# Attention on one core: folding the running maximum to 64 partitions, and where its transposes stand

## The chip, the cores and the metric

The kernel runs on one core of one Trainium2 chip. The metric is the device time of one execution in microseconds (us). The kernel before takes 1297.36 us (median of three runs, 1296.2 to 1297.93). The profile was taken from one further execution, which took 1299.13 us; its span, from the first instruction to the last, is 1296.9 us.

## The reference

The reference is one encoder layer with two groups of token mixing heads over a sequence of 2048 tokens of width 1024: gated linear attention (group A), multi-head latent attention with four heads (group B), one output projection over both, a residual and a layer norm. The change touches group B alone, whose core is a softmax over all 2048 keys:

```python
def attend(blk):
    qn, qr = blk
    s = (jnp.einsum('bqhd,bkhd->bhqk', qn, k_nope, preferred_element_type=jnp.float32)
         + jnp.einsum('bqhr,bkr->bhqk', qr, k_r, preferred_element_type=jnp.float32))
    p = jax.nn.softmax(s, axis=-1)
    return jnp.einsum('bhqk,bkhv->bqhv', p.astype(v.dtype), v)
```

The softmax subtracts, for each query, the largest score over all keys before the exponential.

## The kernel before

Three stages follow one another: group A (about 0 to 470 us of the span), then chunks of projections that overlap it (to about 605 us), then `attention` (L1501), which ends in the output projection, the residual and the layer norm.

**Blocks and pairs.** Attention runs 16 blocks i = 0 to 15, each one head by 512 queries. A block has 8 pairs j = 0 to 7 of key tiles, 2 x 128 keys each. Scores are held with keys on the partitions and queries along the row, so a maximum over keys is a maximum over partitions. Numbers are split into a high and a low part, so that a product takes several matmuls.

For each pair:

- `scores` (L1527, products on L1535 to L1539): ten products on TensorE into a PSUM tile `pS` of two banks. There are two such tiles, so the scores of pair j + 2 can't start until pair j's tile has been read.
- `copy` (L1541): ScalarE copies the tile to SBUF.
- `smax` (L1546, L1554 and L1557): VectorE folds the two halves of the PSUM tile into the running maximum `rm`, 128 partitions by 512 queries. Of the readers of the tile it is the last.
- `sub`, `exp`, `phi`, `plo` (L1578 to L1592): VectorE subtracts the maximum, ScalarE takes the exponential and copies the high part, GpSimd makes the low part `pl`.
- `pv` (L1615): six products of weights and values into `o`.
- `acc` (L1602): half of the pairs are summed on VectorE into `ap`, the others on GpSimd.

Once per block:

- `tmax` (L1559): four TensorE transposes of `rm` into the one-bank PSUM pool `pX`; `rmax` (L1565): one VectorE reduction of them to `mc`; `bmax` (L1570): four TensorE transposes that spread `mc` over all partitions into `mb`, which each `sub` reads.
- `tot`, `own_half`, `fold`, `tsum`, `rcp` (L1625 to L1660): the same for the sum. Here ScalarE copies half of the sum to the other 64 partitions (`own_half`, two instructions of 64 x 256), VectorE adds the halves (`fold`, two of 64 x 256), and only two transposes follow. `keep` stores the reciprocals with a DMA of ScalarE's queue.
- `oh`, `ol`, `y`, `yc` (L1689 to L1706): the block's output is split and multiplied by a value matrix into a tile of `pX`; ScalarE evacuates it and a DMA of SyncE's queue stores it.
- For block 14 `turn` (L1676) takes the place of `keep`: one small transpose of the reciprocals into `pX` on TensorE, then `rows` (L1683), a ScalarE copy and a DMA on SyncE's queue.

**The order is written out by hand.** Every step of every block is put on one list with a place, and the list is sorted. `scores` of pair j of block i has place 8i + j; the other steps of a pair are that place plus the value in `PLACE` (L74); those of a block are 8i + 7 plus it. `PLACE_LAST` (L100) holds for block 15, `PLACE_OUT` for the steps of the output projection. `in_order` (L386) chains each engine's instructions, the DMA queues' included, in exactly this order. So an instruction that waits holds up all that stand behind it on its engine.

Around a block's end, before the change, the list reads (next block's pairs are called p0 to p7): scores of p0; maximum of pair 7; sum of pair 5 on VectorE; `tmax`; value products of pair 4 of the block before; `rmax`; `bmax`; a `phi`; copy of p0; scores of p1; maximum of p0; value products of pair 5; three `sub`; then `tot`, maximum of p1, one `sub`, `fold`, maximum of p2, two `sub`, `ol`, maximum of p3.

Of the kernel before, what the change touches and what calls it, by code (L numbers as in the profile page):

```python
# [9 lines left out]
F32 = mybir.dt.float32  # L10
F32R = mybir.dt.float32r
I32 = mybir.dt.int32
AF = mybir.ActivationFunctionType
ALU = mybir.AluOpType
AX = mybir.AxisListType
# [3 lines left out]
P = 128  # L19
# [8 lines left out]
QB = 512  # L28
# [45 lines left out]
PLACE = dict(  # L74
    copy=0.73,
    max=1.21,
    sub=(9.47, 8.65, 7.39, 7.37, 7.49, 6.63, 6.95, 7.44),
    exp=(10.18, 9.95, 7.63, 9.15, 8.26, 9.12, 7.84, 8.01),
    hi=(10.39, 10.41, 9.81, 10.32, 9.82, 10.74, 10.53, 10.47),
    lo=(11.99, 11.22, 11.21, 12.62, 11.98, 11.51, 10.87, 10.63),  # L80
    pv=(12.35, 12.1, 11.89, 12.65, 12.27, 12.25, 12.14, 11.45),
    acc=(12.45, 11.78, 12.32, 0, 10.57, 11.24, 10.03, 9.22),
    acc0=10.78,
    tmax=1.26,
    rmax=1.27,
    bmax=1.48,
    tot=11.2,
    half=11.7,
    fold=11.95,
    tsum=12.37,  # L90
    rcp=13.55,
    keep=14.21,
    turn=13.6,
    rows=13.65,
    oh=12.34,
    ol=12.99,
    y=16.55,
    yc=16.9,
)
PLACE_LAST = dict(  # L100
    sub=(9.67, 8.74, 8.38, 6.77, 10.45, 3.53, 9.53, 5.55),
    exp=(10.14, 9.35, 10.49, 8.31, 13.01, 14.59, 17.1, 18.05),
    hi=(10.43, 11.83, 12.21, 14.39, 15.18, 22.96, 28.7, 34.03),
# [256 lines left out]
class K:  # L360
# [1140 lines left out]
    def attention(self):  # L1501
        tc, nc = self.tc, self.nc
        mm = nc.tensor.matmul
        V, G, Ac = nc.vector, nc.gpsimd, nc.scalar
        NP = NKT // 2
        with ExitStack() as ctx:
# [4 lines left out]
            pM, pO, pX, pA, pS = bank("pM"), bank("pO"), bank("pX"), bank("pA"), bank("pS", 2)  # L1511
            blocks = [(h, b) for b in range(NQB) for h in range(H)]
            nb = len(blocks)
            stt = [dict(s=[None] * NP) for _ in blocks]
# [31 lines left out]
            def smax(i, j):  # L1546
# [8 lines left out]
                else:  # L1555
                    for e in range(2):
                        V.tensor_tensor(d["rm"], src[:, e], d["rm"], ALU.max)  # L1557

            def tmax(i):  # L1559
                d = stt[i]  # L1560
                d["x"] = pX.tile([P, 4, P], F32, tag="x", name=f"mx{i}")
                for e in range(4):
                    nc.tensor.transpose(d["x"][:, e], d["rm"][:, e * P:(e + 1) * P], self.ident)

            def rmax(i):  # L1565
                d = stt[i]
                d["mc"] = op.sm.tile([P, 4], F32, tag="mc", name=f"mc{i}")
                V.tensor_reduce(d["mc"], d["x"], AX.X, ALU.max)

            def bmax(i):  # L1570

# [53 lines left out]
            def tot(i):  # L1625
# [4 lines left out]
                    return  # L1630
                for e in range(2):
                    V.tensor_tensor(d["ap"], d["ap"], d["as"][:, e], ALU.add)

            halves = [(slice(64 * e, 64 * e + 64), slice(64 - 64 * e, 128 - 64 * e), slice(e * QB // 2, (e + 1) * QB // 2))
                      for e in range(2)]

            def own_half(i):
                d = stt[i]
# [88 lines left out]
            def put(place, fn, *a):  # L1727
                todo.append((place, len(todo), fn, a))

            def at(f, i, j=None):  # L1730
                p = PLACE_LAST.get(f, PLACE[f]) if i == nb - 1 else PLACE[f]
                return p[j] if isinstance(p, tuple) else p

            own = (("tot", tot), ("half", own_half), ("fold", fold), ("tsum", tsum), ("rcp", rcp), ("keep", keep), ("oh", oh), ("ol", ol), ("y", y), ("yc", yc))
            own_late = tuple(e for e in own if e[1] is not keep) + (("turn", turn), ("rows", rows))
            for i in range(nb):
                for j in range(NP):
                    t = NP * i + j
                    put(t, scores, i, j)
                    for n, f in (("copy", copy), ("max", smax), ("sub", sub), ("exp", exp), ("hi", phi), ("lo", plo),  # L1740
                                 ("pv", pv), ("acc", acc)):
                        if n != "acc" or j != SUM_POOL[0] or i == nb - 1:
                            put(t + at(n, i, j), f, i, j)
                put(NP * i + at("acc0", i), acc0, i)
                for n, f in (("tmax", tmax), ("rmax", rmax), ("bmax", bmax)) + {nb - 1: (), nb - 2: own_late}.get(i, own):
                    put(NP * i + NP - 1 + at(n, i), f, i)
                if i + 2 < nb:
                    put(NP * i + 4.05, fetch, i + 2)
# [300 lines left out]
```

## Time and profile before

| What | us |
|---|---|
| median of three runs | 1297.36 |
| the profiled execution | 1299.13 |
| its span | 1296.9 |
| TensorE busy, 0 to 470 us of the span | 457.44 |
| TensorE busy, 470 to 605 us | 133.93 |
| TensorE busy, 605 to 1090 us (blocks 0 to 15) | 483.08 |
| VectorE busy in that stretch | 423.74 |
| ScalarE busy in that stretch | 404.42 |
| GpSimd busy in that stretch | 408.72 |
| TensorE busy, 1090 to 1297 us (output) | 195.76 |

Busy time is the time in which an engine had an instruction running. Matmuls overlap, so the start of one to the start of the next says more than the duration of one. PE is TensorE's matmul, PEld its weight load, DVE is VectorE, ACT ScalarE, POOL GpSimd, SPq SyncE's queue. A timeline row holds the start, the duration, the engine, the line, the operation, output and inputs, the shapes and a count of merged instructions; a bracket at its end gives the idle time just before it and who ended that.

### The profile page before, as it was taken

Reading aid. Unit: us, or ns where it says so; the run is one execution under the profiler, and the core shown is the slowest. Engines: PE = TensorE matmul, PEld = TensorE weight load, DVE = VectorE, ACT = ScalarE, POOL = GpSimd, SP = SyncE. Lnnn points to the kernel's source line nnn. Section 1 sums busy time; section 2 is a strip of 40 time slices with the busy share of each in tenths; the row PEclk is TensorE's granted clock in tenths of the full one; section 3 lists DMA queues with packets and bytes.
Section 4 is the critical chain, followed back from the end, with each engine's and each line's share of the span. In section 5 each row is a group of like instructions: output and inputs, shape, how many; then the busy total and the mean of one; then the engine's idle time right before and its main releaser. Section 6 shows DMA issues by size and latency. Waiting matters only on the chain.

```text
span 1296.9 us, 19995 instructions
## 1 busy us (share of the span) xinstructions
PE 1270.2 (98%) x6988; PEld 1119.6 (86%) x6988; DVE 908.5 (70%) x1678; ACT 842.7 (65%) x1482; POOL 790.9 (61%) x500
## 2 busy tenths in 40 slices
PE   7999999999999999999999999999999999999997
PEld 7999999999889999999788888888888888788886
DVE  6865564445675455555898888888888888468655
ACT  7765657555675656655688888888888887523221
POOL 0243232232567666671288888889999999846550
PEclk9999999999999999999999999999999999999999
DMA  8232213131565555565401111122233110367752
GB/s 287 70 94 59 88 55 93 51 96 50 179 224 170 193 200 179 189 213 168 138 1 41 42 41 41 41 63 60 58 90 90 42 41 9 122 197 238 238 170 75
DMA packets 113444, 145.81 MB, mean 112 GB/s; under 512 B 17494, under 2 KB 70110, under 8 KB 113344
## 3 DMA queue, kind: packets, MB, share of 16 engines
q1 hardware_dynamic: 105184, 142.42, 34.9%
q0 software_dynamic: 768, 2.10, 0.4%
q8 instruction: 55, 0.90, 0.3%
q10 hardware_dynamic: 7392, 0.03, 0.3%
q14 instruction: 45, 0.37, 0.1%
HBM read 94.14 MB, written 50.36 MB: 111 GB/s over the span
## 4 chain that ended last, share of the span: by engine, by line
PE 86%; ACT 3%; DVE 2%; POOL 2%; issue 2%; DMA 1%; SPq 0%; DVEq 0%; ACTq 0%; POOLq 0%
PE o L424 4%; PE o L426 4%; PE pS L1535 4%; PE o L425 4%; PE pS L1537 4%; PE pS L1536 4%; PE pS L1538 4%; PE pS L1539 4%; PE ipa L424 4%; PE ipa L426 3%; PE ipa L425 3%; PE po L426 2%; PE po L425 2%; PE po L424 2%; PE pz L425 2%; PE pz L426 2%
## 5 line engine op out<-in xcount | busy, mean ns | idle before, releaser
L376 POOL TENSOR_TENSOR pl<-s,ph 128x1024 fp32r<-128x1024 f32 x128 | 306.3, 2417 | 58.0 <-ACT ph L370 58.0
L1557 DVE TENSOR_TENSOR rm<-pS,rm 128x512 f32<-128x512 f32 x210 | 144.8, 690 | 26.3 <-ACT s L1544 20.7
L1581 DVE TENSOR_TENSOR s<-s,mb 128x1024 f32<-128x1024 f32 x128 | 151.2, 1213 | 9.4 <-PE mb L1575 9.3
L1544 ACT ACTIVATE s<-pS 128x1024 f32<-128x1024 f32 x128 | 131.3, 1026 | 38.0 <-PE pS L1539 33.4
L1044 POOL TENSOR_TENSOR Us<-Us,cw 128x512 f32<-128x512 f32 x16 | 18.6, 1164 | 213.1 <-DVE Us L1042 181.3
L370 ACT ACTIVATE ph<-s 128x1024 fp32r<-128x1024 f32 x128 | 135.2, 1058 | 17.6 <-PE o L426 16.9
L1585 ACT ACTIVATE s<-s 128x1024 f32<-128x1024 f32 x128 | 131.5, 1051 | 13.4 <-DVE s L1581 13.3
L424 PE MATMUL ipa<-wah,xah 128*128 128x384 f32 (+1 forms) x384 | 131.1, 341 | 7.3 <-ACT wah L370 6.8
L425 PE MATMUL ipa<-wal,xah 128*128 128x384 f32 (+1 forms) x384 | 125.8, 327 | 0.2 <-DVE wal L376 0.2
L426 PE MATMUL ipa<-wah,xal 128*128 128x384 f32 (+1 forms) x384 | 125.0, 325 | 0.0
L1535 PE MATMUL pS<-qh,ckvT_h 128*128 128x512 f32 x256 | 102.5, 401 | 0.8 <-DVE rm L1557 0.4
L424 PE MATMUL o<-ph,vh 128*128 128x512 f32 x256 | 101.0, 395 | 0.0
L1536 PE MATMUL pS<-ql,ckvT_h 128*128 128x512 f32 x256 | 99.8, 390 | 0.0
L1538 PE MATMUL pS<-rh,krs 128*128 128x512 f32 x256 | 99.8, 390 | 0.0
L1537 PE MATMUL pS<-qh,ckvT_l 128*128 128x512 f32 x256 | 99.8, 390 | 0.0
L426 PE MATMUL o<-ph,vl 128*128 128x512 f32 x256 | 99.8, 390 | 0.0
L1539 PE MATMUL pS<-rl,krs 128*128 128x512 f32 x256 | 99.8, 390 | 0.0
L425 PE MATMUL o<-pl,vh 128*128 128x512 f32 x256 | 99.7, 390 | 0.0
L1608 DVE TENSOR_TENSOR ap<-ap,s 128x512 f32<-128x512 f32 x120 | 83.1, 692 | 7.1 <-ACT s L1585 4.5
L424 PEld LDWEIGHTS ipa<-wah,xah 128*128 128x128 f32 x384 | 73.1, 190 | 10.4 <-ACT wah L370 7.0
L376 POOL TENSOR_TENSOR ol<-of,oh 128x512 fp32r<-128x512 f32 x32 | 43.6, 1363 | 54.2 <-ACT oh L370 54.2
L424 PE MATMUL pz<-xch,wzh 128*128 128x256 f32 x256 | 74.8, 292 | 0.0
(327 smaller groups left out, 3830.1 us busy)
## 6 DMA issues: line engine op xcount, KB each, us to landing
xcf<-xT_dram SPq DMA_DIRECT2D x16, 512.0 KB, 5.3
xr<-x_dram SPq DMA_DIRECT2D x16, 512.0 KB, 5.7
out_dram<-rr SPq DMA_DIRECT2D x32, 256.0 KB, 4.9
xaf<-xT_dram SPq DMA_DIRECT2D x14, 512.0 KB, 3.8
oib<-oi_s SPq DMA_DIRECT2D x16, 256.0 KB, 3.8
qdb<-qd_s SPq DMA_DIRECT2D x16, 256.0 KB, 4.9
SU<-su_s SPq DMA_DIRECT2D x16, 256.0 KB, 4.1
ub<-u_s SPq DMA_DIRECT2D x16, 256.0 KB, 4.1
```

The source lines that it names most:

```text
L370: return nc.scalar.activation(dst, src, AF.Copy).ins
L376: return e.tensor_tensor(dst, src, hi.bitcast(F32), ALU.subtract).ins
L424: mm(out, ah, bh, start=start, stop=False)
L425: mm(out, ah, bl, start=False, stop=False)
L426: mm(out, al, bh, start=False, stop=stop)
L1535: mm(ps[:, e], kh, qh, start=True, stop=False)
L1536: mm(ps[:, e], kh, ql, start=False, stop=False)
L1537: mm(ps[:, e], kl, qh, start=False, stop=False)
L1538: mm(ps[:, e], kr, rh, start=False, stop=False)
L1539: mm(ps[:, e], kr, rl, start=False, stop=True)
L1557: V.tensor_tensor(d["rm"], src[:, e], d["rm"], ALU.max)
L1581: V.tensor_tensor(s, s, d["mb"][:, None, :].to_broadcast([P, 2, QB]), ALU.subtract)
```

## The change

For blocks 1 to 14 the running maximum is folded, as the sum already was. `hmax`: ScalarE copies half of `rm` (two instructions of 64 x 256) into the unused half of the PSUM tile of `pX`. `fmax`: VectorE takes the maximum of both halves (two instructions of 64 x 256). `tmax` then makes two transposes instead of four, and `rmax` reduces 256 instead of 512 columns. Blocks 0 and 15 keep the old form and the old places.

The places of the folded blocks move. `tmax` goes from 1.26 to 1.9, behind the six value products at 1.27. `bmax` goes from 1.48 to 2.2, behind the ten score products of p1, which stand between the two. `turn` and `rows` of block 14 move from 13.6 and 13.65 to 17.5 and 17.55: behind 24 output products, `y`, `yc` and the first six value products of block 15.

```diff
-    tmax=1.26,
-    rmax=1.27,
-    bmax=1.48,
+    hmax=1.45,
+    fmax=1.65,
+    tmax=1.9,
+    rmax=1.91,
+    bmax=2.2,
...
-    turn=13.6,
-    rows=13.65,
+    turn=17.5,
+    rows=17.55,
...
+PLACE_FIRST = dict(
+    tmax=1.26,
+    rmax=1.27,
+    bmax=1.48,
+)
 PLACE_LAST = dict(
+    tmax=1.26,
+    rmax=1.27,
+    bmax=1.48,
...
+            folded = lambda i: 0 < i < nb - 1
+
+            def other_half(i):
+                d = stt[i]
+                d["x"] = pX.tile([P, 4, P], F32, tag="x", name=f"mx{i}")
+                f = d["x"][:, 2:4].rearrange("p a t -> p (a t)")
+                for own_p, other_p, qs in halves:
+                    Ac.activation(f[own_p], d["rm"][other_p, qs], AF.Copy)
+
+            def fold_max(i):
+                d = stt[i]
+                f = d["x"][:, 2:4].rearrange("p a t -> p (a t)")
+                for own_p, _, qs in halves:
+                    V.tensor_tensor(d["rm"][own_p, :QB // 2], f[own_p], d["rm"][own_p, qs], ALU.max)
+
             def tmax(i):
                 d = stt[i]
-                d["x"] = pX.tile([P, 4, P], F32, tag="x", name=f"mx{i}")
-                for e in range(4):
+                if not folded(i):
+                    d["x"] = pX.tile([P, 4, P], F32, tag="x", name=f"mx{i}")
+                for e in range(2 if folded(i) else 4):
                     nc.tensor.transpose(d["x"][:, e], d["rm"][:, e * P:(e + 1) * P], self.ident)
 
             def rmax(i):
                 d = stt[i]
                 d["mc"] = op.sm.tile([P, 4], F32, tag="mc", name=f"mc{i}")
-                V.tensor_reduce(d["mc"], d["x"], AX.X, ALU.max)
+                if not folded(i):
+                    V.tensor_reduce(d["mc"], d["x"], AX.X, ALU.max)
+                else:
+                    V.tensor_reduce(d["mc"].rearrange("p (e j) -> p j e", e=2),
+                                    d["x"][:, 0:2].rearrange("p j (e k) -> p j e k", e=2), AX.X, ALU.max)
...
+                fmax = (("hmax", other_half), ("fmax", fold_max)) if folded(i) else ()
+                for n, f in fmax + (("tmax", tmax), ("rmax", rmax), ("bmax", bmax)) + {nb - 1: (), nb - 2: own_late}.get(i, own):
                     put(NP * i + NP - 1 + at(n, i), f, i)
```

More of the change, by code (lines that the diff above doesn't have):

```diff
@@ L1557, in smax @@
                         V.tensor_tensor(d["rm"], src[:, e], d["rm"], ALU.max)
+            halves = [(slice(64 * e, 64 * e + 64), slice(64 - 64 * e, 128 - 64 * e), slice(e * QB // 2, (e + 1) * QB // 2))
+                      for e in range(2)]
+            folded = lambda i: 0 < i < nb - 1
[10 more added lines that the diff above has]
+                    V.tensor_tensor(d["rm"][own_p, :QB // 2], f[own_p], d["rm"][own_p, qs], ALU.max)
             def tmax(i):
                 d = stt[i]
-                d["x"] = pX.tile([P, 4, P], F32, tag="x", name=f"mx{i}")
-                for e in range(4):
+                if not folded(i):
+                    d["x"] = pX.tile([P, 4, P], F32, tag="x", name=f"mx{i}")
+                for e in range(2 if folded(i) else 4):
                     nc.tensor.transpose(d["x"][:, e], d["rm"][:, e * P:(e + 1) * P], self.ident)
@@ L1632, in tot @@
                     V.tensor_tensor(d["ap"], d["ap"], d["as"][:, e], ALU.add)
-            halves = [(slice(64 * e, 64 * e + 64), slice(64 - 64 * e, 128 - 64 * e), slice(e * QB // 2, (e + 1) * QB // 2))
-                      for e in range(2)]
             def own_half(i):
@@ L1730, in at @@
             def at(f, i, j=None):
-                p = PLACE_LAST.get(f, PLACE[f]) if i == nb - 1 else PLACE[f]
+                p = PLACE_LAST.get(f, PLACE[f]) if i == nb - 1 else PLACE_FIRST.get(f, PLACE[f]) if i == 0 else PLACE[f]
                 return p[j] if isinstance(p, tuple) else p
@@ L1744, in attention @@
                 put(NP * i + at("acc0", i), acc0, i)
-                for n, f in (("tmax", tmax), ("rmax", rmax), ("bmax", bmax)) + {nb - 1: (), nb - 2: own_late}.get(i, own):
+                fmax = (("hmax", other_half), ("fmax", fold_max)) if folded(i) else ()
+                for n, f in fmax + (("tmax", tmax), ("rmax", rmax), ("bmax", bmax)) + {nb - 1: (), nb - 2: own_late}.get(i, own):
                     put(NP * i + NP - 1 + at(n, i), f, i)
```

## The prediction

> **What bounds the kernel now.** I read the page's busy times first, then TensorE's waits, then the timeline of one attention block on TensorE and on VectorE.
>
> ```profile
> PE 1270.2 (98%) x6988; PEld 1119.6 (86%) x6988; DVE 908.5 (70%) x1678; ACT 842.7 (65%) x1482; POOL 790.9 (61%) x500
> ```
>
> TensorE bounds the whole: 98% busy. So a change pays only if it takes slots from TensorE, and costs as soon as TensorE waits. TensorE around the end of block 6 (p0 to p7 are the next block's pairs; the first column is the start in us of the span):
>
> ```profile
> 813.89 0.60 PE L1563 MATMUL mx<-ident,rm 128*128 128x128 f32 x4
> ...
> 815.02 0.40 PE L424 MATMUL o<-ph,vh 128*128 128x512 f32 x1
> ...
> 815.72 0.60 PE L1575 MATMUL mb<-ident,mc 128*128 128x128 f32 x4
> ...
> 819.80 0.39 PE L1535 MATMUL pS<-qh,ckvT_h 128*128 128x512 f32 x1
> ...
> 824.79 0.39 PE L1535 MATMUL pS<-qh,ckvT_h 128*128 128x512 f32 x1
> ...
> 827.06 0.38 PE L1658 MATMUL sx<-ident,acc 128*128 128x128 f32 x2
> 827.19 0.48 PE L1535 MATMUL pS<-qh,ckvT_h 128*128 128x512 f32 x1
> 828.43 0.39 PE L1535 MATMUL pS<-qh,ckvT_h 128*128 128x512 f32 x1
> ...
> 830.95 0.39 PE L1535 MATMUL pS<-qh,ckvT_h 128*128 128x512 f32 x1
> ...
> 835.94 0.39 PE L1535 MATMUL pS<-qh,ckvT_h 128*128 128x512 f32 x1
> ...
> 844.78 0.60 PE L1563 MATMUL mx<-ident,rm 128*128 128x128 f32 x4
> ```
>
> No row has a bracket: TensorE never waits here. The scores of p2, p3, p4, p5, p6 start at 819.80, 824.79, 827.19, 830.95, 835.94. Ten products take 2.27 (824.79 to 827.06), so one takes 0.227. VectorE in the same stretch:
>
> ```profile
> 812.23 1.42 DVE L1608 TENSOR_TENSOR ap<-ap,s 128x512 f32<-128x512 f32 x2
> 814.52 0.69 DVE L1568 TENSOR_REDUCE mc<-mx 128x4 f32<-128x512 f32 x1 [0.87 <-PE mx L1563]
> ...
> 816.42 3.48 DVE L1581 TENSOR_TENSOR s<-s,mb 128x1024 f32<-128x1024 f32 x3 [0.59 <-PE mb L1575]
> 819.82 1.43 DVE L1632 TENSOR_TENSOR ap<-ap,acc 128x512 f32<-128x512 f32 x2
> 821.16 1.41 DVE L1557 TENSOR_TENSOR rm<-pS,rm 128x512 f32<-128x512 f32 x2
> 822.48 1.21 DVE L1581 TENSOR_TENSOR s<-s,mb 128x1024 f32<-128x1024 f32 x1
> 823.71 0.86 DVE L1646 TENSOR_TENSOR acc<-ap,acc 64x256 f32<-64x256 f32 x2
> 824.59 1.42 DVE L1557 TENSOR_TENSOR rm<-pS,rm 128x512 f32<-128x512 f32 x2
> 825.93 2.34 DVE L1581 TENSOR_TENSOR s<-s,mb 128x1024 f32<-128x1024 f32 x2
> 828.19 0.68 DVE L376 TENSOR_TENSOR ofl<-o,ofh 128x512 fp32r<-128x512 f32 x1
> 828.79 1.41 DVE L1557 TENSOR_TENSOR rm<-pS,rm 128x512 f32<-128x512 f32 x2
> ...
> 833.70 2.93 DVE L1557 TENSOR_TENSOR rm<-pS,rm 128x512 f32<-128x512 f32 x4
> ...
> 839.53 1.42 DVE L1557 TENSOR_TENSOR rm<-pS,rm 128x512 f32<-128x512 f32 x2 [0.45 <-ACT s L1544]
> ```
>
> From the first subtraction (816.42, which waits for the broadcast `mb`) to the maximum of p3 VectorE has no idle time at all. And the maxima of p1, p2, p3 (L1557) stand in that run: each frees the score tile that p3, p4 and p5 write. Here is a second, hidden clock of the block, and it starts with the broadcast.
>
> **The change part by part.**
>
> *Two transposes fewer.* Four transposes and three value products take 815.02 - 813.89 = 1.13; the three products are 0.68, so the four cost 0.45. Two transposes and five products take 828.43 - 827.06 = 1.37, less 1.13 leaves 0.24. The fold saves 0.21 of TensorE per block, over blocks 1 to 14 **-3.0 us**. Bounds: nothing to 0.45 a block.
>
> *Broadcast ten products later.* Now `mb` starts at 815.72 and the first subtraction 0.70 behind it. On TensorE the scores of p2 and all later work stay in their order behind `mb`; only p1's ten products come to stand ahead of it. Against the scores of p2 and later, VectorE's run therefore starts 2.27 later. How late a score waits once a maximum has ended can be read where block 0 ends, since there VectorE is already late:
>
> ```profile
> 638.00 1.41 DVE L1557 TENSOR_TENSOR rm<-pS,rm 128x512 f32<-128x512 f32 x2
> ```
> ```profile
> 639.55 0.47 PE L1535 MATMUL pS<-qh,ckvT_h 128*128 128x512 f32 x1 [0.42 <-DVE rm L1557]
> 639.86 0.40 PE L1536 MATMUL pS<-ql,ckvT_h 128*128 128x512 f32 x1
> ```
>
> The maximum ends at 639.41; the second product starts at 639.86, so the stream resumes as if at 639.63: 0.22 after the end. With 2.27 + 0.22 = 2.49 added to the end of each maximum:
>
> - p3 needs p1's maximum: 821.16 + 1.41 + 2.49 = 825.06 against 824.79: 0.27 late.
> - p4 needs p2's: 824.59 + 1.42 + 2.49 = 828.50 against 827.19: 1.31 late.
> - p5 needs p3's: 828.79 + 1.41 + 2.49 = 832.69 against 830.95: **1.74 late**.
> - p6 needs p4's, half of the four at 833.70: 835.17 + 2.49 = 837.66 against 835.94: 1.72, within the 1.74 already lost.
>
> So TensorE loses 1.74 per block in three waits of about 0.3, 1.0 and 0.4. Before the change the same check leaves 830.95 - 830.42 = 0.53 of slack at p5, which is why no bracket shows. By the maximum of p6, which today has idle time ahead of it (0.45, waiting for a copy), VectorE is paced by TensorE again; the loss does not build up, but each block pays it anew. Over 14 blocks **+24.4 us**. With the release at 0 instead of 0.22 it would be 1.52, with 0.5 it would be 2.0 a block.
>
> *The fold itself.* It adds two copies on ScalarE and two maxima on VectorE, of the shapes of these groups:
>
> ```profile
> L1646 DVE TENSOR_TENSOR acc<-ap,acc 64x256 f32<-64x256 f32 x4 | 1.7, 421 | 0.1
> L1640 ACT ACTIVATE acc<-ap 64x256 f32<-64x256 f32 x4 | 1.5, 371 | 0.0
> ```
> ```profile
> 812.18 1.06 ACT L370 ACTIVATE ph<-s 128x1024 fp32r<-128x1024 f32 x1
> ...
> 814.08 1.03 ACT L1544 ACTIVATE s<-pS 128x1024 f32<-128x1024 f32 x1 [0.84 <-PE pS L1539]
> ```
>
> The copies (0.74) go ahead of the high part at 812.18, and ScalarE has 0.84 idle behind it, so p0's copy keeps its time, by 0.1. While they wait they hold that high part and p0's copy, which p0's maximum needs only behind the reduction. On VectorE the sum ends at 812.23 + 1.42 = 813.65; the two maxima (0.84) end at 814.49, with the release 814.71. The transposes now stand six products (1.36) behind 813.89, at 815.25: 0.5 to spare. The reduction starts 0.63 behind the transposes (814.52 - 813.89) and takes at most 0.69: 816.6, and the broadcast stands at 815.25 + 0.24 + 2.27 = 817.8. VectorE, waiting for it, has nothing else in its order but p0's maximum. I cost the fold at nothing; without the cover it is up to 0.84 a block.
>
> *The small transpose of block 14.*
>
> ```profile
> 1101.62 0.40 PE L1658 MATMUL sx<-ident,acc 128*128 128x128 f32 x2
> 1105.28 0.27 PE L1680 MATMUL rt<-ident,rc 128*4 128x128 f32 x1 [3.26 <-DVE rc L1669]
> ...
> 1109.61 0.51 PE L424 MATMUL y<-ofh,wv_h 128*128 128x512 f32 x1
> ```
> ```profile
> 1103.90 0.69 DVE L376 TENSOR_TENSOR ofl<-o,ofh 128x512 fp32r<-128x512 f32 x1 [1.00 <-ACT ofh L370]
> ```
> ```profile
> 1106.00:1110.00 4.00, 4.00 (x13) 3.10 (x12) 3.97 (x6) 2.04 (x3) 2.38 (x1) 0.57 0.38 132
> ```
>
> It waits 3.26 for the reciprocal, and then the granted clock (third column from the right) is 0.57. Between 1101.62 and `y` at 1109.61 lie two transposes and twelve products, 0.24 + 2.72 = 2.96 of work in 7.99. Moved back, the products start at once; `y` is then due at 1104.6, its operand ends at 1104.59 and is released by 1104.8. Gain 1109.61 - 1104.8 = **-4.8 us**; bounds 3.3 (the wait alone) and 5.0.
>
> The Trainium skill, "TensorE: Matmul & The Clock Gate", section "What's actually happening", says that an idle window of about 3.4 us halves TensorE's clock and that sustained work restores it. The 0.57 behind 3.26 agrees; by it both parts of the gain go together.
>
> Its reciprocal's store moves on SyncE's queue too:
>
> ```profile
> 1105.88 0.27 SPq L1687 DMA_DIRECT2D r_s<-rt  x1
> 1106.24 0.35 SPq L1848 DMA_DIRECT2D wof<-wO_dram  x1
> ```
>
> The next weight load stood right behind it and comes earlier, which helps `yc`, whose tile the transpose must now wait for.
>
> **Sum:** 24.4 - 3.0 - 4.8 = +16.6 us, on the profiled execution 1299.1 + 16.6 = 1315.7. That execution lies 1.8 above the median of the runs; on the median the forecast is **1314 us**. About 0.2%, 2.6 us, is what a measurement of this kernel can tell from no change.
>
> **The rivals.**
>
> *The lateness is absorbed, faster (0.07).* If p5's scores had at least 2.27 + 0.22 of slack behind p3's maximum, only the savings stay: 1297.4 - 3.0 - 4.8 = 1289.6. It decides at the maximum of p3: today's slack is 0.75 before the release, and VectorE's run has no gap to close. Against it speaks also that block 0's end shows this very wait. For it: the three idle brackets of VectorE show that over a whole block it has time.
>
> *The fold is late (0.08).* If the copies wait behind more of ScalarE's work, the two transposes wait as well. The point is the 0.5 to spare; a fold 1.0 late costs 0.5 a block, 7 us more: 1321. For it: ScalarE's margin is 0.1.
>
> *The short waits lower the clock (0.04).* If three waits per block had the effect of the 3.26 one, each block would run some 4 us at 0.57, 1.7 more, 14 x 1.7 = 24: 1338. Against:
>
> ```profile
> 632.00:644.00 12.00, 10.08 (x46) 7.58 (x46) 10.66 (x13) 9.11 (x10) 2.89 (x2) 1.00 0.11 35
> ```
>
> TensorE is idle for 1.9 of these 12 us in several short waits, and the clock granted is 1.00. The Trainium skill, same page, section "A second HAM failure mode: psum-queue depth-cycling", describes just this: frequent short idle times between groups of matmuls that cycle PSUM make the clock go down and up. It speaks against the change; the row does not bear it out.
>
> *The fold saves nothing, or the waits are shorter (0.03).* Without the 3.0 it is 1317; with half of the delay hidden, 1302.
>
> **How the numbers follow.** My forecast, waits at p3 to p5, has 0.78. Its own range: 1.52 to 2.0 lost, 0.45 to 0 saved per block, 3.3 to 5.0 at the end, gives 1.07 x 14 - 5.0 = +10 to 2.0 x 14 - 3.3 = +24.7, that is 1307 to 1322. I reach up a little for a late fold and down for part of a hidden delay: 1305 to 1324. Faster 0.07, same 0.02, slower 0.91.
>
> **What would show it.** After the change TensorE's waits should name scores (L1535's group) released by VectorE's `rm`, some 14 times three, about 24 us together. From one `mx` to the next it is 30.9 us now (813.89 to 844.78) and should be 32.4. VectorE's idle time ahead of the first subtraction should grow from 0.59 to about 1.5. The wait at `rt` and the 0.57 should be gone. I am wrong if TensorE shows no such waits, if `mx` or `mb` waits, or if the clock falls in the blocks.

## The result and the profile after

The changed kernel takes **1315.5 us** (median of four runs, 1314.9 to 1316.9) against 1297.3 for the kernel before (also four runs): a ratio of 1.0143, with a 95% interval of 1.0128 to 1.0158. The forecast was 1314, range 1305 to 1324. The profiled execution's span is 1315.1, 18.2 more than the 1296.9 before.

The busy times, from the first line of the profile's page:

```profile
PE 1277.8 (97%) x6960; PEld 1112.0 (85%) x6960; DVE 915.5 (70%) x1706; ACT 850.2 (65%) x1510; POOL 791.0 (60%) x500
```

There are 28 matmuls fewer, and yet the span is longer. The list of TensorE's waits (total us, times, longest) holds two groups that are new in this size. Before, the scores waited for a maximum once, 0.4 us, at the end of block 0, and that wait is still among the 15; the value products waited for nothing:

```profile
PE pS L1545 <- DVE rm L1567: 10.1, 15, 0.7
...
PE o L434 <- DVE ofl L386: 3.3, 14, 0.3
```

Line numbers are 10 to 33 higher than before: L1545 is the first score product, L434 the first of a value product, L1592 the transposes of the maximum (`mx`), L1608 the broadcast (`mb`). Here is TensorE's timeline of one block, with the same rows that the prediction shows of the kernel before and the first value product:

```profile
822.82 0.38 PE L1592 MATMUL mx<-ident,rm 128*128 128x128 f32 x2
...
825.33 0.60 PE L1608 MATMUL mb<-ident,mc 128*128 128x128 f32 x4
...
827.16 0.39 PE L1545 MATMUL pS<-qh,ckvT_h 128*128 128x512 f32 x1
...
832.32 0.47 PE L1545 MATMUL pS<-qh,ckvT_h 128*128 128x512 f32 x1
...
834.70 0.38 PE L1688 MATMUL sx<-ident,acc 128*128 128x128 f32 x2
835.77 0.47 PE L1545 MATMUL pS<-qh,ckvT_h 128*128 128x512 f32 x1 [0.69 <-DVE rm L1567]
...
838.53 0.50 PE L434 MATMUL o<-ph,vh 128*128 128x512 f32 x1 [0.25 <-DVE ofl L386]
...
840.02 0.39 PE L1545 MATMUL pS<-qh,ckvT_h 128*128 128x512 f32 x1
...
845.06 0.39 PE L1545 MATMUL pS<-qh,ckvT_h 128*128 128x512 f32 x1
...
855.26 0.38 PE L1592 MATMUL mx<-ident,rm 128*128 128x128 f32 x2
```

The broadcast now stands behind p1's products, and from one `mx` to the next it takes 32.44 us where it took 30.89 (the forecast was 32.4). Counted from the start of p2's scores, the later pairs start:

| scores of | before | after | later by | forecast |
|---|---|---|---|---|
| p3 | 4.99 | 5.16 | 0.17 | 0.27 |
| p4 | 7.39 | 8.61 | 1.22 | 1.31 |
| p5 | 11.15 | 12.86 | 1.71 | 1.74 |
| p6 | 16.14 | 17.90 | 1.76 | 1.74 |

VectorE in the same block:

```profile
826.03 3.48 DVE L1614 TENSOR_TENSOR s<-s,mb 128x1024 f32<-128x1024 f32 x3 [1.64 <-PE mb L1608]
829.43 1.43 DVE L1665 TENSOR_TENSOR ap<-ap,acc 128x512 f32<-128x512 f32 x2
830.77 1.41 DVE L1567 TENSOR_TENSOR rm<-pS,rm 128x512 f32<-128x512 f32 x2
...
834.20 1.42 DVE L1567 TENSOR_TENSOR rm<-pS,rm 128x512 f32<-128x512 f32 x2
...
837.80 0.68 DVE L386 TENSOR_TENSOR ofl<-o,ofh 128x512 fp32r<-128x512 f32 x1
838.40 1.41 DVE L1567 TENSOR_TENSOR rm<-pS,rm 128x512 f32<-128x512 f32 x2
...
850.91 1.42 DVE L1567 TENSOR_TENSOR rm<-pS,rm 128x512 f32<-128x512 f32 x2 [0.85 <-ACT s L1554]
...
855.68 0.42 DVE L1600 TENSOR_REDUCE mc<-mx 128x4 f32<-128x256 f32 x1 [1.26 <-PE mx L1592]
```

The run from the first subtraction to the maximum of p3 takes as long as before (826.03 to 839.81, 13.78; before 816.42 to 830.20, 13.78). It only starts later, behind 1.64 of idle time. So VectorE idles 1.26 + 1.64 around the transposes and the broadcast, where it idled 0.87 + 0.59 before, and a few microseconds on TensorE waits for VectorE. Later in the block VectorE has idle time again (0.85 ahead of the maximum of p7), so the lateness does not grow from block to block.

How the blocks sum up can be read from the start of the first broadcast (block 0) and of the last (block 15). Before, then after:

```profile
L1575 PE MATMUL mb<-ident,mc x64: 270/272/322, 633.9 to 1093.1; 128*128 128x128 f32 x64
```
```profile
L1608 PE MATMUL mb<-ident,mc x64: 270/272/322, 633.7 to 1115.0; 128*128 128x128 f32 x64
```

Between them lie 459.2 us before and 481.3 after: **+22.1 us**, 1.58 for each of the 14 folded blocks. At the end of attention the small transpose's wait is gone, and the clock granted in the stretch around it is 1.00 (the third number from the right in the second view):

```profile
1123.42 0.41 PE L1688 MATMUL sx<-ident,acc 128*128 128x128 f32 x2
...
1126.89 0.47 PE L434 MATMUL y<-ofh,wv_h 128*128 128x512 f32 x1 [0.30 <-DVE rc L1697]
...
1131.77 0.27 PE L1710 MATMUL rt<-ident,rc 128*4 128x128 f32 x1
```
```profile
1112.80:1152.80 40.00, 39.70 (x180) 32.22 (x179) 22.67 (x30) 24.70 (x30) 37.74 (x17) 1.00 0.32 106
```

From the two transposes of the sum to `y` it takes 3.47 where it took 7.99: 4.5 us won. From the last broadcast to the end of the span it takes 200.1 where it took 203.8, so 3.7 of the 4.5 last to the end. With 0.2 less ahead of the first broadcast this gives the span: 22.1 - 3.7 - 0.2 = 18.2.

### The profile page after: what moved, and what is told of

The parts are those of the page before. It is cut to its first block, busy times and chain, and to the rows that moved or that the text cites. A ratio compares the mean times of both kernels' runs of the same rounds, so it can differ in the third digit from the quotient of the medians.

```text
span 1315.1 us, 19997 instructions
## 1 busy us (share of the span) xinstructions
PE 1277.8 (97%) x6960; PEld 1112.0 (85%) x6960; DVE 915.5 (70%) x1706; ACT 850.2 (65%) x1510; POOL 791.0 (60%) x500
## 4 chain that ended last, share of the span: by engine, by line
PE 71%; DVE 14%; issue 5%; ACT 2%; POOL 2%; DMA 1%; SPq 1%; DVEq 0%; POOLq 0%; ACTq 0%
DVE s L1614 6%; PE ipa L434 4%; PE ipa L436 4%; PE ipa L435 4%; PE o L434 3%; PE pS L1545 3%; PE pS L1546 3%; PE pS L1547 3%; PE pS L1548 3%; PE pS L1549 3%; PE o L436 3%; PE o L435 3%; DVE rm L1567 2%; PE pz L435 2%; PE pz L434 2%
## 5 line engine op out<-in xcount | busy, mean ns | idle before, releaser
L434 PE MATMUL ipa<-wah,xah 128*128 128x384 f32 (+1 forms) x384 | 131.0, 341 | 7.3 <-ACT wah L380 6.8
L1545 PE MATMUL pS<-qh,ckvT_h 128*128 128x512 f32 x256 | 103.8, 405 | 10.6 <-DVE rm L1567 10.1
L434 PE MATMUL o<-ph,vh 128*128 128x512 f32 x256 | 102.6, 401 | 3.3 <-DVE ofl L386 3.3
L434 PEld LDWEIGHTS ipa<-wah,xah 128*128 128x128 f32 x384 | 72.8, 190 | 10.4 <-ACT wah L380 7.1
L434 PE MATMUL pz<-xch,wzh 128*128 128x256 f32 x256 | 74.8, 292 | 0.0
```

The lines of the kernel that those rows point to most:

```text
L434: mm(out, ah, bh, start=start, stop=False)
L1545: mm(ps[:, e], kh, qh, start=True, stop=False)
```

## The experiments

The theory: the time is lost because the broadcast, and with it VectorE's gapless run, starts ten products later against the scores, while the run has only 0.53 us of slack at p5. The main rival: the fold's own work on ScalarE and VectorE costs the time. Each experiment ran on one chip beside the kernel before, which took 1297.4 to 1297.9 there.

### The place alone

```diff
 (the kernel before)
-    bmax=1.48,
+    bmax=2.2,
...
+PLACE_FIRST = dict(bmax=1.48)
 PLACE_LAST = dict(
+    bmax=1.48,
...
```

`PLACE_FIRST` and `PLACE_LAST` keep the old place for blocks 0 and 15.

> The kernel before with one number changed: the broadcast of blocks 1 to 14 goes behind the ten score products of p1; no fold, and the small transpose of block 14 stays. Theory (the place costs: VectorE's run starts 2.27 us late against 0.53 of slack): each of 14 blocks loses about 1.75 us, so 1297.3 + 24.5 = 1322, with the waits at p4's scores and at the first value products. Rival (the fold's added copies and maxima cost the time): no change, 1297 to 1298.

Measured: 1322.1, ratio 1.0190 (1.0177 to 1.0204). VectorE's first subtraction, and then TensorE's waits in the same block:

```profile
825.20 3.48 DVE L1583 TENSOR_TENSOR s<-s,mb 128x1024 f32<-128x1024 f32 x3 [2.83 <-PE mb L1577]
```
```profile
834.93 0.47 PE L1537 MATMUL pS<-qh,ckvT_h 128*128 128x512 f32 x1 [0.71 <-DVE rm L1559]
837.70 0.50 PE L426 MATMUL o<-ph,vh 128*128 128x512 f32 x1 [0.26 <-DVE ofl L378]
```

The same two waits stand in the same two places, without any fold. The rival that the fold costs the 22 us falls.

### The small transpose alone

```diff
 (the kernel before)
-    turn=13.6,
-    rows=13.65,
+    turn=17.5,
+    rows=17.55,
```

> The kernel before with only the small transpose of block 14 and its store moved back. Theory: the 3.26 us wait and the slow clock behind it go, 4.5 us as seen at the next product of that stage, less what later waits of the output stage give back: 1293 (1292.5 to 1293.5). Rival (the output stage is paced by its weight transfers, so the time comes back later): 1296 to 1297.3.

Measured: 1292.8, ratio 0.9964 (0.9952 to 0.9977); on another chip 1293.0, 0.9966 (0.9953 to 0.9978). The stretch whose clock was 0.57 before now reads:

```profile
1106.00:1110.00 4.00, 4.00 (x20) 3.20 (x19) 3.90 (x6) 1.93 (x5) 4.00 (x3) 1.00 0.18 66
```

20 matmuls run in these 4 us where 13 ran. The weight transfers don't take the gain back. From the last broadcast to the end the gain is 4.2 us in either run (199.6 against 203.8).

### Half the distance

```diff
 (the kernel after)
-    bmax=2.2,
+    bmax=2.05,
...
-                    put(t, scores, i, j)
+                    if j == 1 and i > 1:
+                        put(t, scores, i, j, (0,))
+                        put(t + 0.1, scores, i, j, (1,))
+                    else:
+                        put(t, scores, i, j)
```

`scores` takes the halves as an argument, so that five products stand ahead of the broadcast and five behind it.

> The kernel after with the broadcast put between the two halves of p1's ten products, so only five stand ahead of it and VectorE's run starts 1.13 us late, not 2.27. Theory (lateness less 0.53 of slack is lost): 0.60 lost and 0.21 saved per block, 0.39 x 14 = +5.5, less 4 for the small transpose: 1298.8. Rival 1 (loss in proportion to the products ahead): 0.88 - 0.21 per block, +9.4 - 4 = 1302.7. Rival 2 (the fold's work costs, the place nothing): 1315 as the kernel after.

Measured: 1299.0, ratio 1.0011 (1.0002 to 1.0020). The broadcasts' first and last start:

```profile
L1610 PE MATMUL mb<-ident,mc x64: 270/273/322, 633.3 to 1098.7; 128*128 128x128 f32 x64
```

Between them lie 465.4 us, 6.2 more than before. That is 0.44 a block, where the theory said 0.39 and proportion 0.67. Half the distance costs 0.65 (0.44 and the 0.21 saved), not half of the 1.79 (1.58 and 0.21) that the whole distance costs: there is a slack, and it is about as large as the rows showed.

### The output's low part earlier

```diff
 (the kernel after)
-    ol=12.99,
+    ol=12.55,
```

> The kernel after with the low part of the output (ol) one subtraction earlier on VectorE, so that the first value products of a block find their PSUM bank free; the maximum of p3 ends when it did. Theory: the 0.25 us bracket at the value products goes and the same lateness shows at p5's scores instead, one product step later: 1315.5, within 1. Rival (the bank of the value products is a cost of its own): 0.5 x 14 = 7 less, 1308.5.

Measured: 1315.3, ratio 1.0133 (1.0117 to 1.0148).

```profile
835.63 0.47 PE L1545 MATMUL pS<-qh,ckvT_h 128*128 128x512 f32 x1 [0.70 <-DVE rm L1567]
839.81 0.47 PE L1545 MATMUL pS<-qh,ckvT_h 128*128 128x512 f32 x1 [0.31 <-DVE rm L1567]
```

The wait at the value products is gone, p5's scores wait instead, 0.31, and the time stays. In the changed kernel `ol` and the maximum of p3 stand next to each other in VectorE's run and are equally late; whichever TensorE needs first shows the wait.

### The fold at the old places

```diff
 (the kernel after)
-    hmax=1.45,
-    fmax=1.65,
-    tmax=1.9,
-    rmax=1.91,
-    bmax=2.2,
+    hmax=1.215,
+    fmax=1.23,
+    tmax=1.26,
+    rmax=1.27,
+    bmax=1.48,
```

> The kernel after with the fold kept but its steps hoisted, so that the two transposes and the broadcast stand at their old places (the copies and maxima right behind the maximum of pair 7, ahead of the sum of pair 5). Theory: no lateness, so the 22 us are gone; the fold itself ends about 0.4 us behind the old slot of the transposes and saves 0.21, so a wait of 0.4 per block shows at mx: 1292.8 (as with the small transpose alone) + 0.2 x 14 = 1295.6. Rival (the fold's work on ScalarE and VectorE costs much wherever it stands): 1310 or more. Rival (the fold is free here): 1289.8.

Measured: 1300.9, ratio 1.0027 (1.0017 to 1.0038). Most of the 22 us are gone, as the theory has it, but the time is 5 us more than I expected. VectorE, then TensorE:

```profile
814.72 0.86 DVE L1585 TENSOR_TENSOR rm<-mx,rm 64x256 f32<-64x256 f32 x2 [0.92 <-ACT mx L1579]
815.61 1.43 DVE L1641 TENSOR_TENSOR ap<-ap,s 128x512 f32<-128x512 f32 x2
817.07 0.42 DVE L1600 TENSOR_REDUCE mc<-mx 128x4 f32<-128x256 f32 x1
```
```profile
815.13 0.39 PE L1549 MATMUL pS<-rl,krs 128*128 128x512 f32 x1
815.72 0.41 PE L1592 MATMUL mx<-ident,rm 128*128 128x128 f32 x2 [0.20 <-ACT ph L380]
815.88 0.48 PE L434 MATMUL o<-ph,vh 128*128 128x512 f32 x1
...
817.55 0.65 PE L1608 MATMUL mb<-ident,mc 128*128 128x128 f32 x4
```

`mx` is due one product behind 815.13, at 815.36, and starts at 815.72: the 0.4 I expected. The bracket names a high part (`ph`), which the transposes don't read. The two maxima of the fold end at 815.58, 0.14 ahead of the transposes, the same distance as in block 14 of g_totfold below, where the bracket does name them (1057.46 + 0.85 = 1058.31, and `mx` at 1058.45); so they are the likelier cause. But I overlooked that the sum of pair 5, which the fold was hoisted past, now stands ahead of the reduction. The reduction ends at 817.49 and the broadcast starts at 817.55, about 0.2 behind the six products. From one `mx` to the next (815.72 to 847.07) it takes 31.35, 0.46 more than before where I expected 0.19; the 0.2 explains most of the difference, and the rest stays open. So at the old places, with only six products between the transposes and the broadcast, the fold's chain costs more than its two transposes bring.

### The sum's additions out of the run

`tot` alone, then `tot` with the sum's fold, moved into VectorE's idle time ahead of the subtractions:

```diff
 (the kernel after; f_tot changes tot alone)
-    tot=11.2,
+    tot=9.8,
-    half=11.7,
-    fold=11.95,
+    half=9.95,
+    fold=10.3,
```

> The kernel after, broadcast behind p1's products as there, but the two additions of tot (1.34 us) moved on VectorE out of the run behind the broadcast into the idle time ahead of it. Theory: the run reaches the maxima only 2.27 - 1.34 = 0.93 late, less 0.53 of slack: 0.40 lost, 0.21 saved per block: 1292.8 + 2.7 = 1295.5. Rival (what counts is when the subtractions start, not what stands between them and the maxima): 1315, as the kernel after.

> As f_tot, and the sum's fold (0.88 us) with its copies on ScalarE moved into the idle time too. Theory: 2.27 - 2.22 = 0.05 late, inside the slack, so nothing is lost and the two transposes saved show: 1292.8 - 3.0 = 1289.8, with no wait at scores or value products of blocks 2 to 15. Rival (two transposes fewer save nothing on TensorE): 1292.8. Rival (the moved additions hold up the reduction and so the broadcast): a wait at mb, 1295 or more.

Measured: with `tot` alone (f_tot) 1299.1, ratio 1.0013 (1.0004 to 1.0022); with the fold of the sum as well (g_totfold) 1291.5, ratio 0.9955 (0.9942 to 0.9967). The rival that the start of the subtractions counts falls: they start behind the late broadcast as in the changed kernel, and 16 and 24 us come back.

In f_tot VectorE has:

```profile
819.21 3.48 DVE L1614 TENSOR_TENSOR s<-s,mb 128x1024 f32<-128x1024 f32 x3 [1.47 <-PE mb L1608]
822.61 1.41 DVE L1567 TENSOR_TENSOR rm<-pS,rm 128x512 f32<-128x512 f32 x2
823.94 1.21 DVE L1614 TENSOR_TENSOR s<-s,mb 128x1024 f32<-128x1024 f32 x1
...
826.23 1.42 DVE L1567 TENSOR_TENSOR rm<-pS,rm 128x512 f32<-128x512 f32 x2 [0.20 <-ACT s L1554]
```

This is the larger part of why it came out 3.6 us above the 1295.5: the maximum of p2 now has to wait 0.20 for its copy, which stands on ScalarE behind exponentials that also start with the subtractions. Taking work out of VectorE's run uncovers ScalarE's. Between the broadcasts this is worth 2.3 us of the 3.6 (464.2, so +5.0, where +2.7 was expected). The rest lies behind the last broadcast, where TensorE's list names 0.4 us at the sum's transposes and 0.4 at an output product that the small transpose alone doesn't have; it was not tested by a run.

In g_totfold, TensorE from one `mx` to the next, and VectorE in the block before:

```profile
843.07 0.38 PE L1592 MATMUL mx<-ident,rm 128*128 128x128 f32 x2
...
873.74 0.38 PE L1592 MATMUL mx<-ident,rm 128*128 128x128 f32 x2
```
```profile
811.58 1.43 DVE L1665 TENSOR_TENSOR ap<-ap,acc 128x512 f32<-128x512 f32 x2
...
814.10 0.86 DVE L1676 TENSOR_TENSOR acc<-ap,acc 64x256 f32<-64x256 f32 x2
815.54 3.48 DVE L1614 TENSOR_TENSOR s<-s,mb 128x1024 f32<-128x1024 f32 x3 [0.58 <-PE mb L1608]
...
821.90 1.42 DVE L1567 TENSOR_TENSOR rm<-pS,rm 128x512 f32<-128x512 f32 x2 [0.40 <-ACT s L1554]
...
826.09 1.41 DVE L1567 TENSOR_TENSOR rm<-pS,rm 128x512 f32<-128x512 f32 x2
```

The block takes 30.67, by 0.22 less than 30.89: the two transposes saved now show. The idle time ahead of the subtractions is used, down from 1.64 to 0.58. The margin is thinner than I expected, though. From the first subtraction to the end of the maximum of p3 it takes 11.96 where it took 13.78: 1.82 less, and not 2.22, since the maximum of p2 waits 0.40 for ScalarE's copy. So VectorE is still 2.27 - 1.82 = 0.45 late, and not 0.05; that is just inside the slack of about 0.5.

Not all of the 3.0 arrives. In block 14 the moved addition waits for GpSimd's sum, and the transposes, whose fold stands ahead of that addition in the list, start 0.2 late too:

```profile
1058.57 1.43 DVE L1665 TENSOR_TENSOR ap<-ap,acc 128x512 f32<-128x512 f32 x2 [0.27 <-POOL acc L1646]
```
```profile
1058.45 0.41 PE L1592 MATMUL mx<-ident,rm 128*128 128x128 f32 x2 [0.23 <-DVE rm L1585]
```

Behind the last broadcast one value product of block 14 waits 0.5 for a low part from GpSimd, which neither the small transpose alone nor the changed kernel shows:

```profile
PE o L435 <- POOL pl L386: 0.5, 1, 0.5
```

### The two best side by side

> The small transpose alone once more, on one chip with g_again: ratio to the kernel before 0.9964.

> The kernel with the fold, the late broadcast and the sum's additions in VectorE's idle time once more. If the two transposes saved show in full it lies 3.0 us below b_again, 0.9941; if nothing of them is left at the end, level with it.

Measured on one chip: the small transpose alone 1293.0 (1292.7 to 1294.0), ratio 0.9966 (0.9953 to 0.9978); with the fold and the sum's additions moved 1291.6 (1291.2 to 1291.8), ratio 0.9953 (0.9940 to 0.9965). No run of the one reaches the other's range, so about half of the 3.0 is there: between expectation and nothing. The kernel with the additions moved lies 24 us below the changed kernel and 6 below the one before; about 4.5 of the 6 come from the small transpose.

## Why the prediction was right

- **TensorE pays for waits and is paid for slots.** Right, and the sign followed from it.
- **Two transposes fewer, 0.21 a block.** Right where nothing hides it: 0.22 in g_totfold, and the place alone costs 24.9 us between the broadcasts (484.1) where the change costs 22.1, a difference of 2.8 against the 3.0 forecast.
- **Broadcast ten products later, 1.74 a block.** Right: 1.71 at p5, 1.76 at p6. The half distance and the two moved additions show that what counts is the lateness less the slack.
- **Three waits, at p3, p4 and p5.** Wrong in the third. The block's first value products wait first, 0.25, because `ol` must have read their PSUM bank; the prediction checked the score tiles for a release by VectorE, and not the bank of `o`. Before the change the product that needs it started here:

```profile
829.59 0.39 PE L424 MATMUL o<-ph,vh 128*128 128x512 f32 x1
```

`ol` ended at 828.19 + 0.68 = 828.87, so with the 0.22 for the release this slack was 0.50, against 0.53 at p5: 2.27 - 0.50 = 1.77 late, the 1.76 that p6 shows. That the missed release hardly moved the total is luck: the two slacks happen to be nearly the same.
- **About 24 us of waits in the list.** Wrong as a sign to look for: the brackets give 10.1 + 3.3. Matmuls are shown with 0.39 each while they follow at 0.227, so some 0.16 of each wait lies under the previous matmul's bar, and p3's lateness of 0.17 shows no bracket at all. The starts show all of it.
- **The fold at nothing.** Right in its place: it ends 0.84 ahead of the transposes (853.57 + 0.85 against 855.26). Less the 0.22 for the release that leaves 0.6, where 0.5 to spare was forecast.

```profile
853.57 0.85 DVE L1585 TENSOR_TENSOR rm<-mx,rm 64x256 f32<-64x256 f32 x2
```

- **The small transpose, -4.8.** The direction right, the size a little high: 4.5 at `y`, 3.7 behind the last broadcast; alone it gave 4.2 there. The traces put 1.1 of what the forecast was too low to this term and 0.7 to the blocks (22.1 against 24.4 - 3.0 = 21.4). One later wait of the output stage is new:

```profile
1199.83 0.50 PE L436 MATMUL pmb<-woh,ol 128*128 128x512 f32 x1 [0.19 <-POOL ol L386]
```

- **The rival of the falling clock.** Not borne out: each folded block has two waits of up to 0.7, and the granted clock of the stretch stays at 1.00:

```profile
605.00:1110.00 505.00, 489.97 (x2188) 391.79 (x2187) 429.93 (x610) 410.37 (x484) 407.28 (x179) 1.00 0.21 56
```

## What to carry to other kernels

When an instruction is moved back on a saturated engine, look at what the other engine does behind it: here VectorE's gapless run from the broadcast to the maxima that free the score tiles. Work out each release in it, of every bank and not only of the score tiles, against the start that needs it; the loss is the lateness less the smallest slack. Here half the distance cost about a third of the whole (0.65 against 1.79). If the late place is wanted, use the idle time that it opens on the other engine: work taken out of the run and put there brought back what the late place cost, and about half of what the fold saves. Look then at what the shorter run uncovers, here ScalarE's copy.

## What the runs showed of the hardware

TensorE's granted clock went to half around the one wait of 3.26 us. In the kernel before, that wait ends at 1105.28; the clock was 1.00 up to 1106.4, 0.50 from 1106.5 to 1109.8 and 1.00 again from 1109.9. The kernel with the place alone has the same wait (3.25 us, up to 1127.97); there the clock was 1.00 up to 1127.3, 0.50 from 1127.5 to 1130.8 and 1.00 again from 1130.9. So it stayed at half for about 3.4 us both times, but once from 1.2 us after the end of the wait and once from 0.6 us before it: how much work fell into the slow stretch differed between the two. Behind some thirty waits of 0.2 to 0.7 us in the changed kernel it did not move.

A transpose of 128 x 128 in a stream of such products cost a slot of about 0.11 us (four took 0.45, two 0.24), well below the 0.27 that its row shows.
